# The down product of an MLP by seven products of quadrants: operands prepared in the stage before and kept in DRAM

## The chip, the cores and the metric

The kernel runs on one core of one Trainium2 chip. The core has five engines with queues of their own: TensorE (PE in the profile, PEld its weight loads), VectorE (DVE), ScalarE (ACT), GpSimd (POOL) and SyncE (SP). Transfers between DRAM and on-chip memory are issued from the queues of SP, ACT and POOL. The metric is the device time of one execution in microseconds.

## The reference

One decoder layer on 2048 tokens of width 1024. The part around the change is the gated MLP, with a depthwise convolution of width 3 over the tokens ahead of the activation (D_FF = 2816 = 22 x 128):

```python
h = h + jnp.concatenate([att, pool], axis=-1) @ w_out[i]
hn = _rmsnorm(h, ln_ffn[i])
up = _causal_dwconv(hn @ w_up[i], conv_w[i], conv_b[i])
gate, val = jnp.split(up, 2, axis=-1)
h = h + (jax.nn.silu(gate) * val) @ w_down[i]
g = jax.nn.sigmoid(_rmsnorm(h, ln_ple[i]) @ w_ple_gate[i])
h = h + g * (p[i] @ w_ple[i])
```

Ahead of it stand the input projection, a dilated sliding-window attention and a multi-scale pooling; behind it a last RMSNorm. All numbers are float32.

## The kernel before

Everything is kept transposed: features on the 128 partitions, tokens along the row. The 2048 tokens are four chunks of 512 (`CH`) or two halves of 1024.

**Split products.** TensorE multiplies in the type fp32r. `split` writes a number as a high part (ScalarE casts it, L84) and a low part (a subtraction on VectorE or GpSimd, L85), and `mm3` makes of one product three matmuls: high x high (L89), low x high (L90), high x low (L91). Each is 128x128 weights by 128x512 tokens.

**Up product** (930 to 1782 us of the profiled execution). For one half and one f (one of 22 blocks of 128 columns, for gate and value together) it multiplies two 2 x 2 block matrices by seven products in place of eight, in Winograd's form: the operands are quadrants a11, a12, a22 of the normed input, sums s1 to s4 of its quadrants, quadrants b11, b21, b22 of the weights and sums t1 to t4. Such a (half, f) is a *turn*: 7 x 4 x 3 = 84 matmuls (`product`, L1315). The split inputs of a half stay on chip in pools `opa` and `opb`. The sums t are made by GpSimd in the first half and kept in DRAM for the second. `prepare` norms the inputs of a half, makes s1 to s4 and stores them to DRAM (tiles `nt`); `Refill` fetches them again around the change of halves (the *half boundary*, turns `NF - 1`, `NF` and `NF + 1`), some fetches ahead, and splits them (`L1371`, `L1372`). A turn's products go into the banks ua, ub, uc; VectorE adds them up in `ug` and `uv` (`add`, L1338). One turn later the convolution (L1328 to L1335), ScalarE's silu and a product on VectorE (L1512) make `yg`, 128 x 1024, which is stored to `g.act`.

**Down product** (1782 to 2273 us). A loop over four chunks of tokens (c) and 22 blocks f; for each, 512 KB of weights and 256 KB of activations are loaded (`rd`, `ra`, SP's queue) and split, and `mm3` adds to eight output tiles of 128 x 512 (`dn`). The eighth output lags by `wait` = 5 blocks. A chunk closes with `closed(j)`: the old h, loaded from DRAM, plus the bank, stored to `h2`, and its square for the statistics of the next norm. The first three pairs of weights and activations are loaded and split by `first_units` inside the last turns of the up product.

**Gate phase** (2273 to 2519 us). The gate's and the embedding's products, the last norm and the output.

**What sets the order.** Within each engine's queue the instructions stand in the order written, with semaphores between engines; a buffer of a pool is taken again when its last reader is done. Inside the up product the place is given by slots: `after(slot)` is called seven times a turn, and `splits(slot)` puts the weights' splits behind certain products. In the down product `ahead(n + 3)` and `act_ahead(n + 3)` issue loads and splits three units ahead.

## Time and profile before

| | us |
|---|---|
| runs: lowest, median, highest of 3 | 2516.77, 2523.27, 2527.26 |
| profiled execution | 2522.12 |
| its span in the profile | 2519.8 |
| granted TensorE clock, mean | 0.98 |
| TensorE busy | 2407.5 (96% of the span) |
| VectorE, ScalarE, GpSimd busy | 1588.8, 1108.6, 515.7 |
| HBM read and written | 290.01 MB and 131.89 MB |

A row of a timeline has the start and the duration in us, the engine, line and operation, output<-inputs, shapes, and in brackets how long the engine was idle just before it and what it had waited for. A row of a group has the total of busy time, the mean of one instruction in ns, and the group's idle time by releaser. A row of windows has, for a stretch of time, the busy time and (x) instructions of each engine, the granted TensorE clock, the busy share of the DMA engines and what they moved. A row of DMA issues has the queue, the count, the size of one and the median time from issue to landing in us.

### The profile page before, as it was taken

To read this page: it belongs to the slowest core of one execution; us is meant where nothing else is said; L and a number is where in the kernel's file an instruction comes from. 1 tells how busy PE (TensorE), PEld (TensorE's weight loads), DVE (VectorE), ACT (ScalarE), POOL (GpSimd) and SP (SyncE) were. 2 spreads that over 40 slices of the span, in tenths; PEclk is the share of its full clock that TensorE was granted. 3 is DMA by queue.
4 is the path that set the end of the run, shared out by engine and by line. 5 is a ranking of instruction groups with operands and counts; after the bars stand their busy time and mean duration, and the time that the engine had idled before them with its cause. 6 is when DMAs were issued, how large, how long until landed. Compare 5 with 4: busy or idle time off the path is not lost.

```text
span 2519.8 us, 31897 instructions
## 1 busy us (share of the span) xinstructions
PE 2407.5 (96%) x11515; PEld 2022.4 (80%) x11515; DVE 1588.8 (63%) x2416; ACT 1108.6 (44%) x1923; POOL 515.7 (20%) x423
## 2 busy tenths in 40 slices
PE   8999998888779999999999999999999999999998
PEld 7888887777767877888887888888788888887888
DVE  6635427777774467888888666666535374435755
ACT  5423326887751135544446444444323242323322
POOL 3312221053430023333340000000122222221000
PEclk9999999999879999999999999999999999999999
DMA  7534358687646674555556334333546464635332
GB/s 240 174 120 180 142 178 248 166 193 180 164 164 221 223 252 167 167 177 181 175 194 211 122 117 138 121 114 117 191 134 222 149 219 150 208 122 173 124 105 88
DMA packets 209052, 424.08 MB, mean 168 GB/s; under 512 B 42464, under 2 KB 68896, under 8 KB 205824
## 3 DMA queue, kind: packets, MB, share of 16 engines
q1 hardware_dynamic: 170576, 368.41, 46.4%
q0 software_dynamic: 18672, 25.88, 3.1%
q10 hardware_dynamic: 19648, 27.77, 3.1%
q8 instruction: 90, 1.47, 0.2%
q14 instruction: 66, 0.54, 0.1%
HBM read 290.01 MB, written 131.89 MB: 167 GB/s over the span
## 4 chain that ended last, share of the span: by engine, by line
PE 79%; DMA 6%; DVE 6%; issue 3%; ACT 2%; POOL 0%; SPq 0%; ACTq 0%; POOLq 0%; DVEq 0%
PE ua L1315 18%; PE uc L1315 9%; PE dn L90 6%; PE dn L91 6%; PE dn L89 6%; PE ub L1315 4%; PE z L91 4%; PE z L89 4%; PE z L90 4%; PE o L89 2%; PE o L91 2%; PE o L90 2%; PE gp L89 2%; PE gp L91 2%; PE gp L90 2%
## 5 line engine op out<-in xcount | busy, mean ns | idle before, releaser
L89 PE MATMUL dn<-ah,hd 128*128 128x512 f32 x704 | 275.3, 391 | 2.8 <-ACT ah L84 2.8
L90 PE MATMUL dn<-al,hd 128*128 128x512 f32 x704 | 274.9, 391 | 1.7 <-DVE al L85 1.7
L91 PE MATMUL dn<-ah,ld 128*128 128x512 f32 x704 | 274.6, 390 | 0.0
L85 POOL TENSOR_TENSOR ld<-rd,hd 128x1024 fp32r<-128x1024 f32 x42 | 100.9, 2403 | 812.8 <-ACT hd L84 812.8
L84 ACT CAST hd<-rd 128x1024 fp32r<-128x1024 f32 x88 | 92.5, 1052 | 266.3 <-PE dn L90 230.9
L85 DVE TENSOR_TENSOR al<-ra,ah 128x512 fp32r<-128x512 f32 x88 | 116.8, 1330 | 136.0 <-ACT ah L84 136.0
L89 PE MATMUL z<-hnh,wh 128*128 128x512 f32 (+1 forms) x480 | 170.3, 355 | 9.9 <-ACT hnh L252 5.8
L90 PE MATMUL z<-hnl,wh 128*128 128x512 f32 (+1 forms) x480 | 170.0, 354 | 2.7 <-DVE hnl L253 2.6
L91 PE MATMUL z<-hnh,wl 128*128 128x512 f32 (+1 forms) x480 | 169.9, 354 | 2.3 <-POOL wl L85 1.7
L89 PEld LDWEIGHTS dn<-ah,hd 128*128 128x128 f32 x704 | 132.7, 188 | 31.0 <-ACT ah L84 3.2
L90 PEld LDWEIGHTS dn<-al,hd 128*128 128x128 f32 x704 | 132.7, 188 | 29.8 <-DVE al L85 2.2
L91 PEld LDWEIGHTS dn<-ah,ld 128*128 128x128 f32 x704 | 132.7, 189 | 27.4
L85 DVE TENSOR_TENSOR wu<-ru,wu 128x1024 fp32r<-128x1024 f32 x88 | 127.4, 1448 | 0.0
L155 DVE TENSOR_TENSOR acc<-acc,sq 128x512 f32<-128x512 f32 (+1 forms) x125 | 90.2, 722 | 47.6 <-ACT sq L154 34.6
L1315 PE MATMUL uc<-a22h,wu 128*128 128x512 f32 x352 | 115.7, 389 | 1.8 <-DVE uv L1338 1.8
L1315 PE MATMUL ua<-s2h,wu 128*128 128x512 f32 x352 | 115.8, 390 | 1.1 <-ACT ug L1452 1.1
L1315 PE MATMUL uc<-s3h,wu 128*128 128x512 f32 x352 | 116.2, 390 | 0.3 <-ACT s3h L1371 0.3
L1315 PE MATMUL ub<-a12h,wu 128*128 128x512 f32 x352 | 115.9, 390 | 0.3 <-ACT a12h L1371 0.3
L1315 PE MATMUL ua<-s4h,wu 128*128 128x512 f32 x352 | 115.5, 389 | 0.0
L1315 PE MATMUL ua<-s1h,wu 128*128 128x512 f32 x352 | 115.5, 389 | 0.0
L1315 PE MATMUL ua<-a11h,wu 128*128 128x512 f32 x352 | 115.5, 389 | 0.0
L85 DVE TENSOR_TENSOR ld<-rd,hd 128x1024 fp32r<-128x1024 f32 x46 | 56.2, 1223 | 89.1 <-ACT hd L84 89.1
(317 smaller groups left out, 6474.4 us busy)
## 6 DMA issues: line engine op xcount, KB each, us to landing
rd<-in_w_down_dram SPq DMA_DIRECT2D x88, 512.0 KB, 3.6
ru<-in_w_up_dram SPq DMA_DIRECT2D x66, 512.0 KB, 4.1
ra<-act SPq DMA_DIRECT2D x88, 256.0 KB, 3.8
act<-yg SPq DMA_DIRECT2D x43, 512.0 KB, 3.1
wr<-in_w_in_dram SPq DMA_DIRECT2D x64, 256.0 KB, 4.0
nt<-h SPq DMA_DIRECT2D x56, 256.0 KB, 3.9
h<-h SPq DMA_DIRECT2D x56, 256.0 KB, 5.6
td<-t SPq DMA_DIRECT2D x22, 512.0 KB, 2.6
```

What stands on the lines that cost most here:

```text
L84: nc.scalar.copy(hi, src)
L85: (low or nc.gpsimd).tensor_tensor(lo, src, fp(hi), op=ALU.subtract)
L89: nc.tensor.matmul(ps, wh, ah, start=first, stop=False)
L90: nc.tensor.matmul(ps, wh, al, start=False, stop=False)
L91: nc.tensor.matmul(ps, wl, ah, start=False, stop=last)
L155: nc.vector.tensor_tensor(acc[:, :n], acc[:, :n], sq[:, :n], op=ALU.add)
L1315: nc.tensor.matmul(pst, x[:, ksl], y, start=first and k == 0 and n == 0, stop=k == HK - 1 and n == 2, skip_group_check=True)
```

## The change

The down product becomes, for each half of 1024 tokens, seven products of quadrants like the up product's. Its rows are two chunks of tokens, its columns two halves of the 1024 outputs, and the sum over f is cut into the pairs (q, q + 11), q = 0 to 10. A *unit* is now one pair in one product: 12 matmuls on 256 KB of weights and 256 KB of activations. The seven products follow one another in `SEQ`, each over all 11 pairs, in two sets of four banks, A and B; some products go on adding to a bank that an earlier one has begun, and after each product its four banks are added to h as they stand.

The activations' quadrants and sums are made in the up product: the turns go in pairs (q, q + 11), and after the second one of a pair `results` stores a11, a12 and a22 and puts four subtractions or additions on VectorE for s1 to s4, stored to `g.oq`. The sums of the down weights are made by GpSimd in 11 turns of the second half (`down_sums`), with loads and stores on its own queue, and kept in `g.dd`. The normed inputs of `prepare` and `Refill` have four buffers where they had six, the fetches ahead are four and six instead of six and ten, and `prepare` for the second half begins in turn 3. The stores of the last pair, a11's apart, go to GpSimd's queue.

```diff
-        turns = [(half, f) for half in range(2) for f in range(NF)]
+        turns = [(half, f) for half in range(2) for q in range(NP) for f in (q, q + NP)]
...
-                        t[q] = pool.tile([P, CH], F32, tag="nt", bufs=6, name="nt")
+                        t[q] = pool.tile([P, CH], F32, tag="nt", bufs=nnt, name="nt")
...
-        FETCH = (("nt", 6), ("inv", 2), ("dg", 2))
+        FETCH = (("nt", 4), ("inv", 2))
...
-            nc.sync.dma_start(raw, rows(w_down, n))
+            nc.sync.dma_start(raw, w_down[n * P : (n + 1) * P, :CH])
...
+        def keep(half, p, q, t):
+            (nc.gpsimd if half and q == NP - 1 and p != "a11" else nc.sync).dma_start(g.oq[half][p][q], t)
+
+        def results(pr):
+            if pr.f < NP:
+                keep(pr.half, "a11", pr.f, pr.yg[:, lo_])
+                first_f[0] = pr.yg
+                return
+            q, half, one, two = pr.f - NP, pr.half, first_f[0], pr.yg
+            keep(half, "a12", q, two[:, lo_])
+            keep(half, "a22", q, two[:, hi_])
+            x = fp(fb.tile([P, CH], F32R, tag="dg", bufs=2, name="x"))
+
+            def sums_13():
+                nc.vector.tensor_tensor(x, one[:, hi_], two[:, hi_], op=ALU.add)
+                keep(half, "s1", q, x)
+                nc.vector.tensor_tensor(one[:, hi_], one[:, lo_], one[:, hi_], op=ALU.subtract)
+                keep(half, "s3", q, one[:, hi_])
+
+            def sum_2():
+                nc.vector.tensor_tensor(x, x, one[:, lo_], op=ALU.subtract)
+                keep(half, "s2", q, x)
+
+            def sum_4():
+                nc.vector.tensor_tensor(two[:, lo_], two[:, lo_], x, op=ALU.subtract)
+                keep(half, "s4", q, two[:, lo_])
+
+            sums.extend([[0, sums_13], [2, sum_2], [4, sum_4]])
...
+        def down_sums(q):
+            b = []
+            for r in (w_down[q * P : (q + 1) * P, :], w_down[(q + NP) * P : (q + NP + 1) * P, :]):
+                for x in range(2):
+                    t = fb.tile([P, CH], F32, tag="nt", bufs=4, name="nt")
+                    nc.gpsimd.dma_start(t, r[:, x * CH : (x + 1) * CH])
+                    b.append(t)
+
+            def rest():
+                b11, b12, b21, b22 = b
+                for n, (o, x, y) in enumerate(((b11, b12, b11), (b12, b22, b12), (b22, b22, b11), (b21, b21, b22))):
+                    nc.gpsimd.tensor_tensor(o, x, y, op=ALU.subtract)
+                    nc.gpsimd.dma_start(g.dd[q][("t1", "t3", "t2", "t4")[n]], o)
...
-            refill = Refill(0, ("a12", "s3", "a22"), 6)
+            refill = Refill(0, ("a12", "s3", "a22"), 4)
...
-                    (nc.gpsimd if over else nc.sync).dma_start(g.act[prev.f][:, prev.half * 1024 : prev.half * 1024 + 1024], prev.yg)
+                    results(prev)
...
+                if over:
+                    unit[4]()
+                    while sums:
+                        due_sums()
...
+        SEQ = (
+            ("a11", "b11", True, True, (0, 0)),
+            ("a12", "b21", False, True, (0, 0)),
+            ("s2", "t2", True, False, (1, 0)),
+            ("s3", "t3", False, True, (1, 1)),
+            ("s1", "t1", True, False, (1, 1)),
+            ("a22", "t4", False, False, (1, 0)),
+            ("s4", "b22", True, False, (0, 1)),
+        )
+        order = [(half, n, q) for half in range(2) for n in range(len(SEQ)) for q in range(NP)]
...
+                rw = fd.tile([P, CH], F32, tag="rw", bufs=4, name="rw")
+                nc.sync.dma_start(rw, weights(SEQ[x][1], q))
+                ra = fd.tile([P, CH], F32, tag="ra", bufs=4, name="ra")
+                nc.sync.dma_start(ra, g.oq[half][SEQ[x][0]][q])
+                w = wtile()
+                split(nc, w[:, :CH], w[:, CH:], rw, nc.vector)
...
+                split(nc, ah, al, ra, nc.vector)
...
+        for n, (half, x, q) in enumerate(order):
+            pa, wb, chain, starts, (row, col) = SEQ[x]
+            mine = "AB"[(half + (not chain)) % 2]
...
+            ahead(n + 4)
+            if n >= len(order) - 8 and n % 2 == len(order) % 2 and len(gates) < NW:
+                gates.append(load_w(rows(w_gate, len(gates)), f"g{len(gates)}", nc.vector))
+            if x in (0, 2, 3, 6) and q in (2, 4, 6, 8):
+                j = (q - 2) // 2
+                ht = fd.tile([P, CH], F32, tag="h", bufs=18, name="h")
+                c = 2 * half + row
+                nc.sync.dma_start(ht, g.h1[4 * col + j][:, c * CH : (c + 1) * CH])
...
+            for j in range(4):
+                js = slice(j * P, (j + 1) * P)
+                mm3(nc, banks[mine][j], wh[:, js], wl[:, js], ah, al, starts and q == 0, q == NP - 1, not starts)
+                if q == NP - 1:
+                    ht = htiles[half, row, col, j]
+                    nc.vector.tensor_tensor(ht, ht, banks[mine][j], op=ALU.add)
+                    if x in (1, 4, 5, 6):
+                        c = 2 * half + row
+                        nc.scalar.dma_start(g.h2[4 * col + j][:, c * CH : (c + 1) * CH], ht)
```

The rows below are instructions in the order of an engine's queue: line, operation, output<-inputs, shape. From L1342 of the kernel before on, the lines of the changed one are 4 and more higher; where before has `add` at L1338, the changed one has it at L1342, and its L1338 is a row of the convolution.

VectorE at the half boundary, the kernel before: the low parts of the refilled inputs (`s4l`, `a22l`) stand between the turn's own work.

```order
L1372 TENSOR_TENSOR s4l_12502<-nt,s4h_12501 128x512
L1338 TENSOR_TENSOR uv<-uv,uc 128x512
L1512 TENSOR_TENSOR yg<-yg,yv 128x1024
L85 TENSOR_TENSOR wu<-ru_12135,wu 128x1024
L85 TENSOR_TENSOR wu<-t_12323,wu 128x512
L1372 TENSOR_TENSOR a22l_12533<-nt,a22h_12532 128x512
L1372 TENSOR_TENSOR a22l_12537<-nt,a22h_12536 128x512
L1372 TENSOR_TENSOR a22l_12562<-ninv,a22h_12561 128x512
L1372 TENSOR_TENSOR a22l_12566<-ninv,a22h_12565 128x512
L1328 SCALAR_TENSOR_TENSOR yv<-uv,vec,yv 128x1023
```

The same place with the change; `x` is the tile of s1 and s2, `yg` the results of the pair.

```order
L1376 TENSOR_TENSOR s4l_12774<-ninv,s4h_12773 128x512
L1342 TENSOR_TENSOR uv<-uv,uc 128x512
L1581 TENSOR_TENSOR yg<-yg,yv 128x1024
L85 TENSOR_TENSOR wu<-ru_12395,wu 128x1024
L85 TENSOR_TENSOR wu<-t_12587,wu 128x512
L1376 TENSOR_TENSOR a22l_12807<-nt,a22h_12806 128x512
L1376 TENSOR_TENSOR a22l_12811<-nt,a22h_12810 128x512
L1418 TENSOR_TENSOR x<-yg 128x512
L1420 TENSOR_TENSOR yg<-yg 128x512
L1376 TENSOR_TENSOR a22l_12840<-nt,a22h_12839 128x512
L1376 TENSOR_TENSOR a22l_12844<-nt,a22h_12843 128x512
L1332 SCALAR_TENSOR_TENSOR yv<-uv,vec,yv 128x1023
```

Two of the pair's sums stand between the second and the third `a22l`.

VectorE where the up product ends, the kernel before: the convolution and the product of the last turn, and the splits of the down product's units three and four (`ld`, `al`).

```order
L1328 SCALAR_TENSOR_TENSOR yg<-ug,vec,yg 128x1023
L85 TENSOR_TENSOR ld_3_15458<-rd_3_15455,hd_3_15457 128x1024
L1329 SCALAR_TENSOR_TENSOR yg<-ug,vec,yg 128x1022
L1334 SCALAR_TENSOR_TENSOR yg<-halo,vec,yg 128x1
L1335 SCALAR_TENSOR_TENSOR yg<-halo,vec,yg 128x2
L1512 TENSOR_TENSOR yg<-yg,yv 128x1024
L85 TENSOR_TENSOR ld_5_15526<-rd,hd_5_15525 128x1024
```

With the change, from the same product on:

```order
L1581 TENSOR_TENSOR yg<-yg,yv 128x1024
L1418 TENSOR_TENSOR x<-yg 128x512
L1420 TENSOR_TENSOR yg<-yg 128x512
L85 TENSOR_TENSOR wu<-rd,wu 128x512
L85 TENSOR_TENSOR al<-ra,ah 128x512
L1424 TENSOR_TENSOR x<-x,yg 128x512
L1428 TENSOR_TENSOR yg<-yg,x 128x512
L85 TENSOR_TENSOR wu<-rw,wu 128x512
L85 TENSOR_TENSOR al<-ra,ah 128x512
```

The fifth unit's two splits stand between the pair's first two sums and its last two, and the sixth unit's (`rw`) behind all four.

SP's queue at the same place, with the semaphores that each transfer waits for (DMASW: transfers issued by GpSimd, DMAHW: by SP or ACT). Before:

```order
L1544 DMA rd<-in_w_down_dram 128x1024 [waits DMAHW6_49,DMAHW3_49,DVE_49]
L1544 DMA rd<-in_w_down_dram 128x1024 [waits DMAHW7_49,DMAHW5_49,Pool_49]
L1559 DMA ra<-act_208 128x512 [waits DMAHW0_49,DVE_49]
L1559 DMA ra<-act_209 128x512 [waits DMAHW1_49]
L1614 DMA h<-h_227 128x512 [waits DVE_49]
L1559 DMA ra<-act_210 128x512
```

With the change; `rg` are the gate's weights, `rd` the fifth unit's weights:

```order
L1386 DMA rd<-in_w_down_dram 128x512 [waits DMAHW2_49,DMAHW0_49,DVE_49]
L954 DMA rg_19694<-in_w_gate_dram 128x1024 [waits DMAHW6_49,DMAHW1_49,DVE_49]
L954 DMA rg_19748<-in_w_gate_dram 128x1024 [waits DMAHW0_49,DVE_49]
L1630 DMA rw<-in_w_down_dram 128x512 [waits DMAHW3_49]
L1632 DMA ra<-oq0a_210 128x512 [waits DMASW2_49,DMASW1_49,DMAHW4_49,DMASW0_49,Pool_49]
L1676 DMA h<-h_403 128x512 [waits DMAHW5_49,DMASW7_49,DVE_49]
L1630 DMA rw<-in_w_down_dram 128x512 [waits DMASW2_49]
L1632 DMA ra<-oq0a_211 128x512 [waits DMAHW7_49]
```

Two loads of the gate's weights now stand ahead of the sixth unit's, and the first load of h, which waits for a store of GpSimd's queue and for VectorE, ahead of the seventh's.

More of the change, by code (lines that the diff above doesn't have):

```diff
@@ L1520, in phase_rest @@
         pctx.close()
-        wait = 5
-        NX = 3
         dctx = ExitStack()
@@ L1635, in phase_rest @@
         aux[0] = db
-        ahead(len(order))
-        wg = [units.pop(("g", 0, k)) for k in range(NW)]
+        wg = gates
         wg += [load_w2(db, rows(w_gate, k), f"wg{k}", nc.vector) for k in range(NW, KD)]
@@ L1799, in tile_layer @@
     g.td = per(NF, [P, S], F32, "td")
-    g.act = per(NF, [P, S], F32, "act")
+    g.oq = [{p: per(NF // 2, [P, CH], F32, f"oq{h}{p}") for p in ("a11", "a12", "a22", "s1", "s2", "s3", "s4")} for h in range(2)]
+    g.dd = [{p: dr.tile([P, CH], F32, tag=f"dd{q}{p}", name=f"dd{q}{p}") for p in ("t1", "t2", "t3", "t4")} for q in range(NF // 2)]
     g.h1 = per(KD, [P, S], F32, "h1")
```

198 lines of the change are left out of this document (98 added, 100 removed).

## The prediction

> **What bounds the kernel now.** I read the page's busy line and its chain first, then the stages one by one, then the groups of the down product and the DMA issues.
>
> ```profile
> PE 2407.5 (96%) x11515; PEld 2022.4 (80%) x11515; DVE 1588.8 (63%) x2416; ACT 1108.6 (44%) x1923; POOL 515.7 (20%) x423
> ...
> PE 79%; DMA 6%; DVE 6%; issue 3%; ACT 2%; POOL 0%; SPq 0%; ACTq 0%; POOLq 0%; DVEq 0%
> ```
>
> TensorE is busy for 96% of the span and carries 79% of the chain. So fewer matmuls shorten the time, wherever nothing else becomes late. The stages, in order the first and second half of the up product, the down product, the gate phase, and then a stretch with the heaviest traffic of the down product:
>
> ```profile
> core 0: us, PE busy (x) PEld busy (x) DVE busy (x) ACT busy (x) POOL busy (x), PEclk, DMA share, GB/s
> 925.00:1358.00 433.00, 427.06 (x1872) 349.86 (x1871) 360.35 (x366) 215.34 (x270) 149.80 (x84) 1.00 0.53 179
> 1358.00:1784.00 426.00, 424.20 (x1870) 350.60 (x1869) 299.02 (x375) 213.06 (x264) 0.00 (x0) 1.00 0.39 129
> 1784.00:2273.00 489.00, 483.74 (x2134) 399.66 (x2133) 227.05 (x216) 161.50 (x215) 109.01 (x47) 0.99 0.55 179
> 2273.00:2519.00 246.00, 233.07 (x1261) 201.25 (x1259) 143.88 (x244) 77.81 (x139) 22.60 (x18) 0.98 0.36 119
> 2030.00:2060.00 30.00, 29.22 (x133) 24.06 (x132) 23.15 (x25) 15.90 (x24) 8.78 (x4) 1.00 0.88 290
> ```
>
> All four stages are TensorE's, at a granted clock of 0.98 to 1.00. The down product takes 489 us with some 5 us of idle TensorE, so only the number of its matmuls is to be had there.
>
> ```profile
> L89 PE MATMUL dn<-ah,hd 128*128 128x512 f32 x704 | 275.3, 391 | 2.8 <-ACT ah L84 2.8
> ...
> L84 ACT CAST ah<-ra 128x512 fp32r<-128x512 f32 x88 | 53.7, 615 | 13.5 <-DMA ra<-act 13.5
> ...
> L85 DVE TENSOR_TENSOR al<-ra,ah 128x512 fp32r<-128x512 f32 x88 | 116.8, 1330 | 136.0 <-ACT ah L84 136.0
> ```
>
> The row shows 704 matmuls, a third of the three forms, 2112 in all. Its 391 ns is not the price of one: 2112 x 0.391 = 826 us would not fit into 489 us, since matmuls overlap. The price is the step from one to the next. A turn of the up product has 7 x 4 x 3 = 84 matmuls of the same shape, and VectorE's same add comes back one turn later:
>
> ```profile
> 1160.12 0.69 DVE L1338 TENSOR_TENSOR ug<-ug,ub 128x512 f32<-128x512 f32 x1 [1.94 <-PE ub L1315]
> ...
> 1179.16 0.69 DVE L1338 TENSOR_TENSOR ug<-ug,ub 128x512 f32<-128x512 f32 x1 [1.41 <-PE ub L1315]
> ```
>
> (1179.16 - 1160.12) / 84 = 0.2267 us. By it the down product is 2112 x 0.2267 = 478.8 us; the rest of the 489 us is the stall at its start and its statistics.
>
> **Removed matmuls.** Seven products of 11 pairs, 4 outputs and 3 split terms are 924 matmuls in a half, 1848 in both: 264 fewer, as the order of TensorE's rows also has it. 264 x 0.2267 = 59.9 us, **-59.9**. A unit (one pair in one product) is 12 matmuls, 2.72 us.
>
> **Can the loads and splits keep up with 2.72 us?** Before, 24 matmuls (5.44 us) needed 768 KB; now 12 need 256 KB of weights and 256 KB of activations, 524,288 / 2.72 = 193 GB/s. Weights and activations were 88 x 0.786 = 69 MB of the stage's 179 x 489 = 87.5 MB; with 154 x 0.524 = 81 MB instead it is 99 MB in some 430 us, 231 GB/s, and by the stage's own share 0.55 x 231/179 = 0.71. The stretch at 2030 carried 290 GB/s at a share of 0.88 with TensorE busy for 29.2 of 30 us.
>
> ```profile
> rd<-in_w_down_dram SPq DMA_DIRECT2D x88, 512.0 KB, 3.6
> ...
> ra<-act SPq DMA_DIRECT2D x88, 256.0 KB, 3.8
> ...
> h<-h SPq DMA_DIRECT2D x56, 256.0 KB, 5.6
> ...
> mh<-mh POOLq DMA_DIRECT2D x12, 256.0 KB, 2.7
> ...
> qll<-ql SPq DMA_DIRECT2D x16, 512.0 KB, 14.3
> ```
>
> A buffer is taken from the issue to the landing (3.8, at worst h's 5.6) and 0.62 + 0.69, with the hop between them 1.4 us, for cast and subtraction, 5.2 to 7.0 us; four buffers allow 10.9. The splits, without GpSimd now, are 2 x 0.615 on ScalarE and 2 x 0.69 on VectorE in 2.72 us. That VectorE's `al` shows 1330 ns is GpSimd's doing, which leaves (0.69 in a row at 1802.68 below, without it). The closing adds rise from 32 to 56, 24 x 0.69 = 17 us of VectorE, beside TensorE, and each has a whole product (30 us) before its bank is used again. I take **0**; the ends are 0 and the second rival's price.
>
> The Trainium skill speaks against such loads: "DMA: Bandwidth & Descriptors", section "Rules for kernel authors", wants 128 partitions and at least 1 MiB per DMA for full bandwidth. Its section "Anatomy of one DMA — SWDGE (gpsimd) path" gives 2.0 us + bytes/436e3 on GpSimd's queue, by which I estimate 2.6 us for 256 KB and, one after another, 308 x 2.6 = 801 us. This trace agrees that half the size does not halve the landing (3.6 and 3.8 us), and not that they go one after another: 7.4 us of landings fitted into each 5.44 us. By the page the stage would be 801 us; by the rows the term is 0, and the page's case goes with rival 2.
>
> **The start of the down product.** Now its first matmul is at 1782.48 and it stalls 2.81 + 1.67 = 4.5 us for the fourth unit:
>
> ```profile
> 1782.48 0.39 PE L89 MATMUL dn<-ah,hd 128*128 128x512 f32 x1
> ...
> 1799.74 0.79 PE L89 MATMUL dn<-ah,hd 128*128 128x512 f32 x1 [2.81 <-ACT ah L84]
> 1802.20 0.80 PE L90 MATMUL dn<-al,hd 128*128 128x512 f32 x1 [1.67 <-DVE al L85]
> ```
>
> VectorE at that place:
>
> ```profile
> 1786.19 1.22 DVE L85 TENSOR_TENSOR ld<-rd,hd 128x1024 fp32r<-128x1024 f32 x1
> ...
> 1793.10 2.52 DVE L1512 TENSOR_TENSOR yg<-yg,yv 128x1024 f32<-128x1024 f32 x1 [1.19 <-ACT yg L1502]
> ...
> 1802.68 0.69 DVE L85 TENSOR_TENSOR al<-ra,ah 128x512 fp32r<-128x512 f32 x1 [0.54 <-ACT ah L84]
> ```
>
> With the change four units are ready, so the fifth is needed at 1782.5 + 4 x 2.72 = 1793.4. On VectorE the last product `yg<-yg,yv` comes 1.75 us earlier (ahead of it stand two splits of 0.69 instead of two of 1.22 and one of 0.69), so at 1791.35, and ends at 1792.6 without GpSimd beside it, then x and s3 to 1794.0, then the fifth unit's splits to 1795.3: a stall of 1.8. The sixth unit's load stands on SP's queue behind two loads of gate weights, which wait for the split buffers of units four and five; it is issued at about 1795.7 and ready at 1795.7 + 3.8 + 1.4 = 1800.9, needed at 1797.9: 3.0. The seventh's stands behind the first load of h, which waits for the last s2's store on GpSimd's queue (s1's store at 1794.3, landing 2.7 by `mh`, sum, store, landing 2.7: about 1801); 1801 + 3.8 + 1.4 = 1806.2 to 1806.8 against 1803.6: 3.2. Together 8.0 for 4.5: **+3.5**. Ends: 0 with landings of 2.6, +11 if all of them take h's 5.6.
>
> **The half boundary.** VectorE has no gap there, and two of its splits already end late or nearly so:
>
> ```profile
> 1376.87 0.50 PE L1315 MATMUL ua<-s4l,wu 128*128 128x512 f32 x1 [1.68 <-DVE s4l L1372]
> ...
> 1383.21 1.29 DVE L1372 TENSOR_TENSOR a22l<-ninv,a22h 128x512 fp32r<-128x512 f32 x2
> ```
>
> The fourth sum of the pair before lengthens the 1.68 by 0.7; the sums x and s3 of the last pair (1.2) and it put the last two `a22l` 1.8 us later, ready at 1385.6, needed at 1384.0 after a11's product: 1.6. **+2.3**, between 0.7 and 4. A matmul that waits on TensorE is not made up for later.
>
> **The first refill** (six fetches ahead become four). ScalarE waits there already, and TensorE with it:
>
> ```profile
> 947.35 0.62 ACT L1371 CAST s3h<-nt 128x512 fp32r<-128x512 f32 x1 [5.25 <-DMA nt<-op0s]
> ```
>
> Two fetches less ahead means an issue up to one slot (2.7 us) later behind the same 5.25: **+1**, from -1 to +3.
>
> **The sums in the up product.** In each second turn of a pair VectorE gets four more 128x512, 4 x 0.69 = 2.8 us. By the stage rows its idle time in the first half is (433 - 360) / 22 = 3.3 us a turn; the two adds above alone waited 1.94 and 1.41 us for TensorE. The light turn after it has the same again, and adds are late by at most a product (2.7 us) before a bank is missed. In the second half it idles (426 - 299) / 22 = 5.8 us a turn, but GpSimd's 44 subtractions are new there. In the first, 149.8 us of GpSimd went with 360 us of VectorE against 299 without; 44 of 149.8 / 84 = 1.8 us are 78, so 61 x 78/149.8 = 32 us more, 2.9 in each of 11 turns, and 2.9 + 2.8 stand against 5.8. **0**; up to 16 (1.5 us in each of 11 turns). The stores (1.75 MB for a pair, 1 MB before) run in 38 us at shares of 0.39 to 0.53: 0. Six of the last pair's seven stores move from SP's queue to GpSimd's: none but the h load above waits for them.
>
> **The gate phase.** Its weights come up inside the last eight units and its last closing has four adds instead of a train of eight: **0**, -3 to +3.
>
> **Sum.** -59.9 + 3.5 + 2.3 + 1 = -53.1. The profiled execution took 2522.1, so 2469.0; the median of the runs is 1.2 us above it: **2470**.
>
> **Rivals.** (1) VectorE falls behind in the second turns of the first half, because GpSimd slows its sums as it slows the splits there: 1 to 2 us in each of 11 turns, 2481 to 2491. For it: 2.8 us against 3.3, which contention (the 1330 ns of `al` against 690) would turn; against it: the light turn after. (2) The other side: the down product waits for its loads. The point is a cycle of 12.2 us per buffer (4 x (2.72 + 52/154)); above it the matmuls saved are spent. With `qll`'s 14.3 us (14.3 + 1.3)/4 = 3.9 us a unit, 154 x 3.9 = 601, and 2522 - 491 + 601 = 2632. For it: four pairs of 256 KB in flight, more requests; against it: 3.8 us at share 0.55, and the stretch at 290 GB/s. In part it gives 2491 to 2510. (3) The start is covered, and its 4.5 us go too: 2452 to 2460. That the matmuls do not fall is excluded by the order.
>
> **Chances.** The forecast 0.72 (its own range 2460 to 2482), rival 1 0.10, rival 3 0.05, loads late in part 0.03, about as before 0.05, slower 0.05. Less than 0.5% (2511 to 2536) can't be told from no change here. Faster 0.90, same 0.05, slower 0.05. The range takes the forecast, rival 1 and half of rival 3: 2455 to 2491.
>
> **What would show it.** Down product near 1848 x 0.2267 + 8 = 427 us plus statistics, with no wait for `rw` or `ra` after its first 25 us; the landing of `rw` and `ra` under 6 us; three stalls of 1.8, 3.0 and 3.2 us at its start; `s4l` at 2.4 and `a22l` at 1.6 us at the boundary; up turns still at 19.04 us. Wrong it would be by landings above 9 us in the down product, or by turns of 20 us where the sums are.

## The result, and the profile after

The changed kernel takes 2463.97 us (median of 4 runs, 2457.80 to 2468.53) against 2522.39 (4 runs, 2516.77 to 2527.26): the ratio is 0.9774, with a 95% interval from 0.9755 to 0.9793. It was forecast at 2470, from 2455 to 2491. The profiled execution took 2463.29 us, span 2461.2. Its busy line, a form of the down product's matmuls, and the loads:

```profile
PE 2345.0 (95%) x11251; PEld 1969.5 (80%) x11251; DVE 1723.8 (70%) x2705; ACT 1147.7 (47%) x2055; POOL 528.9 (21%) x515
...
L89 PE MATMUL dn<-ah,wu 128*128 128x512 f32 x616 | 240.8, 391 | 5.3 <-ACT ah L84 5.3
...
rw<-in_w_down_dram SPq DMA_DIRECT2D x61, 256.0 KB, 4.0
...
h<-h SPq DMA_DIRECT2D x56, 256.0 KB, 5.2
```

264 matmuls fewer (11515 to 11251), each group of the down product 616 where it had 704, and more work on VectorE and ScalarE. The stages by windows:

```profile
core 0: us, PE busy (x) PEld busy (x) DVE busy (x) ACT busy (x) POOL busy (x), PEclk, DMA share, GB/s
925.00:1358.00 433.00, 428.12 (x1876) 351.29 (x1876) 394.68 (x408) 217.40 (x271) 155.10 (x84) 1.00 0.59 195
1358.00:1784.00 426.00, 419.32 (x1839) 344.18 (x1838) 360.05 (x416) 207.95 (x259) 114.76 (x132) 1.00 0.61 203
1784.00:2214.00 430.00, 422.57 (x1864) 348.56 (x1863) 267.79 (x420) 204.16 (x350) 6.10 (x9) 1.00 0.72 235
```

The down product moves 235 GB/s at a share of 0.72 (231 and 0.71 were forecast). The second half of the up product has lost some 5 us of TensorE (424.2 to 419.3).

Windows cut at fixed times mix stages a little, so the balance below goes by starts of matmuls: the first of the up product, the first and the last of the down product, the last of all.

```profile
1788.33 0.39 PE L89 MATMUL dn<-ah,wu 128*128 128x512 f32 x1
...
2220.69 0.39 PE L91 MATMUL dn<-ah,wu 128*128 128x512 f32 x1
```

The table does this for each run, from its profiled execution. "Over" is what the turns take beyond 19.04 us each: the 22 turns of the first half, the two at the half boundary, and the others of the second half.

| kernel | up product | first half over | boundary over | second half over | down product | gate phase |
|---|---|---|---|---|---|---|
| before | 851.8 | 8.9 | 2.4 | 0.0 | 490.2 | 239.7 |
| changed | 858.1 | 8.1 | 4.8 | 4.7 | 432.4 | 233.3 |
| e1 eighth product | 861.3 | 7.9 | 6.0 | 7.0 | 492.7 | 233.2 |
| e2 two buffers | 859.2 | 9.7 | 4.9 | 4.0 | 439.9 | 233.9 |
| e3 half more loads | 862.7 | 9.5 | 6.2 | 6.5 | 433.8 | 233.2 |
| e4 start unit | 861.1 | 10.7 | 5.4 | 4.6 | 433.8 | 233.2 |
| e5 start memory | 858.2 | 8.1 | 5.7 | 3.9 | 427.1 | 233.3 |
| e6 light turns | 861.8 | 8.0 | 5.6 | 7.7 | 426.3 | 233.3 |
| e7 no subtractions | 854.3 | 8.2 | 5.6 | 0.0 | 432.9 | 233.2 |
| e8 no sums | 856.5 | 10.7 | 5.4 | 0.0 | 430.7 | 233.5 |
| e9 even turns | 865.0 | 11.6 | 5.7 | 7.2 | 427.2 | 233.2 |
| e10 gates late | 862.4 | 9.5 | 4.8 | 7.5 | 432.8 | 233.2 |
| e11 no sums, deep | 851.7 | 8.8 | 2.4 | 0.0 | 430.8 | 234.1 |
| e12 other tile | 856.2 | 7.8 | 5.2 | 2.8 | 426.9 | 233.2 |

From before to changed: up product +6.3, down product -57.9, gate phase -6.4, the rest (0.4 ahead of the first matmul, 0.1 behind the last) -0.5, together -58.6, which is the difference of the spans. Each row is one execution. The rows that have the same code in a stage, or nearly so, show how far one execution differs from the next there. For changed, e1 to e6, e9 and e10 it is 7.9 to 11.6 us over in the first half (5.8 to 9.6 of it in the first turn), 4.8 to 6.2 at the boundary and 3.9 to 7.7 in the second half, and the changed kernel's own execution stands near the low end of each. In the gate phase it is less than 1 us.

At the start of the down product TensorE's waits in the changed kernel are three, on units five, six and seven, as forecast:

```profile
1801.35 0.50 PE L90 MATMUL dn<-al,wu 128*128 128x512 f32 x1 [1.75 <-DVE al L85]
...
1808.27 0.62 PE L89 MATMUL dn<-ah,wu 128*128 128x512 f32 x1 [4.13 <-ACT ah L84]
1814.34 0.49 PE L89 MATMUL dn<-ah,wu 128*128 128x512 f32 x1 [1.22 <-ACT ah L84]
```

SP's queue beside them: the two loads of the gate's weights take from 1792.75 to 1801.05, and the sixth unit's `rw` comes behind them; the load of h goes out at 1808.35, and the seventh's `rw` behind it.

```profile
1792.75 8.30 SPq L954 DMA_DIRECT2D rg<-in_w_gate_dram  x2
1801.10 0.60 SPq L1630 DMA_DIRECT2D rw<-in_w_down_dram  x1
...
1808.35 0.33 SPq L1676 DMA_DIRECT2D h<-h  x1
1808.72 0.42 SPq L1630 DMA_DIRECT2D rw<-in_w_down_dram  x1
```

In the up product, behind its first turn, five of TensorE's waits of over 0.5 us are new, and a sixth, on `s4l`, stood at the boundary before too (1.68 us). Three are at the boundary, three in the second half:

```profile
1363.73 0.50 PE L1319 MATMUL ua<-s2h,wu 128*128 128x512 f32 x1 [0.92 <-ACT ug L1520]
1376.82 0.50 PE L1319 MATMUL ua<-s4l,wu 128*128 128x512 f32 x1 [1.65 <-DVE s4l L1376]
1385.24 0.50 PE L1319 MATMUL uc<-a22l,wu 128*128 128x512 f32 x1 [0.87 <-DVE a22l L1376]
...
1479.69 0.50 PE L1319 MATMUL uc<-a22h,wu 128*128 128x512 f32 x1 [0.53 <-DVE uv L1342]
1551.68 0.50 PE L1319 MATMUL ua<-s4h,wu 128*128 128x512 f32 x1 [0.56 <-ACT uv L1567]
1559.32 0.50 PE L1319 MATMUL uc<-a22h,wu 128*128 128x512 f32 x1 [1.90 <-DVE uv L1342]
```

The forecast had the one on `s4l` at 2.4 and the one on `a22l` at 1.6; the first, behind a copy of ScalarE, and the last three, in which VectorE is late, it had at nothing. The last three stand in the stretch in which GpSimd subtracts:

```profile
1385.00:1562.00 177.00, 173.69 (x761) 142.46 (x761) 166.43 (x164) 80.15 (x98) 113.60 (x130) 1.00 0.79 269
1562.00:1784.00 222.00, 221.95 (x979) 183.48 (x978) 167.21 (x217) 107.37 (x132) 0.00 (x0) 1.00 0.43 142
```

The program writes the 44 subtractions into 11 turns, up to turn 34 of turns 0 to 43. GpSimd runs ahead of that: the first starts at 1389.5, the last at 1554.7, in turn 31, and behind them it has nothing to do up to the down product. VectorE is busy for 166 of 177 us in that stretch, and for 167 of 222 us behind it, where no turn is late.

### The profile page after: what moved, and what is told of

Same layout as the page of the kernel before. It is cut to its first block, busy times and chain, and to the rows that moved or that the text cites. A ratio compares the mean times of both kernels' runs of the same rounds, so it can differ in the third digit from the quotient of the medians.

```text
span 2461.2 us, 32489 instructions
## 1 busy us (share of the span) xinstructions
PE 2345.0 (95%) x11251; PEld 1969.5 (80%) x11251; DVE 1723.8 (70%) x2705; ACT 1147.7 (47%) x2055; POOL 528.9 (21%) x515
## 4 chain that ended last, share of the span: by engine, by line
PE 73%; DVE 10%; DMA 8%; issue 3%; ACT 2%; POOL 0%; SPq 0%; DVEq 0%; POOLq 0%; ACTq 0%
PE ua L1319 15%; PE uc L1319 7%; PE dn L90 5%; PE dn L89 5%; PE dn L91 5%; PE ub L1319 4%; PE z L91 4%; PE z L89 4%; PE z L90 4%; PE o L91 2%; PE o L89 2%; PE o L90 2%; PE gp L89 2%; PE gp L90 2%; PE gp L91 2%
## 5 line engine op out<-in xcount | busy, mean ns | idle before, releaser
L89 PE MATMUL dn<-ah,wu 128*128 128x512 f32 x616 | 240.8, 391 | 5.3 <-ACT ah L84 5.3
L90 PE MATMUL dn<-al,wu 128*128 128x512 f32 x616 | 240.6, 391 | 2.1 <-DVE al L85 2.0
L91 PE MATMUL dn<-ah,wu 128*128 128x512 f32 x616 | 240.2, 390 | 0.0
L85 DVE TENSOR_TENSOR al<-ra,ah 128x512 fp32r<-128x512 f32 x154 | 105.9, 690 | 109.0 <-ACT ah L84 108.8
L84 ACT CAST ah<-ra 128x512 fp32r<-128x512 f32 x154 | 95.2, 621 | 143.1 <-PE dn L91 133.9
L110 POOL TENSOR_TENSOR pw<-ms,mhalf 128x4 f32<-128x4 f32 (+1 forms) x18 | 17.9, 995 | 636.3 <-ACT ms L108 636.3
L89 PEld LDWEIGHTS dn<-ah,wu 128*128 128x128 f32 x616 | 115.9, 188 | 30.3 <-ACT ah L84 6.2
L90 PEld LDWEIGHTS dn<-al,wu 128*128 128x128 f32 x616 | 116.0, 188 | 27.1 <-DVE al L85 3.2
L91 PEld LDWEIGHTS dn<-ah,wu 128*128 128x128 f32 x616 | 116.0, 188 | 24.2
L85 DVE TENSOR_TENSOR wu<-ru,wu 128x1024 fp32r<-128x1024 f32 x88 | 133.4, 1516 | 1.8 <-ACT wu L84 1.8
L85 DVE TENSOR_TENSOR wu<-rw,wu 128x512 fp32r<-128x512 f32 x149 | 101.1, 688 | 23.5 <-ACT wu L84 23.4
L89 PEld LDWEIGHTS z<-hnh,wh 128*128 128x128 f32 x480 | 94.0, 196 | 21.3 <-ACT hnh L252 5.8
```

What stands on the lines that cost most here:

```text
L84: nc.scalar.copy(hi, src)
L85: (low or nc.gpsimd).tensor_tensor(lo, src, fp(hi), op=ALU.subtract)
L89: nc.tensor.matmul(ps, wh, ah, start=first, stop=False, skip_group_check=again)
L90: nc.tensor.matmul(ps, wh, al, start=False, stop=False, skip_group_check=again)
L91: nc.tensor.matmul(ps, wl, ah, start=False, stop=last, skip_group_check=again)
L110: nc.gpsimd.tensor_tensor(pw[:, :nj], ms[:, :nj], g.mhalf[:, :nj], op=ALU.pow)
```

## The experiments

Kernels e1 to e4 shared one chip and its runs of the kernel before, e5 to e8 another set, e9 to e11 another; e12 ran by itself. A ratio is always to the kernel before, and e7, e8 and e11 ran once.

**e1: an eighth product.** It closes nothing, and its result is not used.

```diff
             ("s4", "b22", True, False, (0, 1)),
+            ("a11", "b11", False, True, (0, 1)),
         )
...
-                if q == NP - 1:
+                if q == NP - 1 and x < 7:
```

> The changed kernel with an eighth product of 11 units in each half (a11 times b11 once more, into the free set of banks, added to nothing): 264 matmuls more, the number of the kernel before, in the new staging; 22 more units of loads and splits come with them. Theory (the matmuls are the gain, 0.2267 us each, and everything that the new staging adds is hidden but for some 2 us): 2464 + 60 = 2524 us, 2519 to 2529, level with the kernel before. Rival (a part of the 58 us came from elsewhere, such as GpSimd's splits that are gone): the extra product then costs less than 50 us, under 2514. Rival (loads near their limit): over 2535, with waits for rw or ra.

2527.1 us, ratio 1.0020 (1.0006 to 1.0033). The down product takes 492.7 us, 60.3 more than the changed kernel's: 60.3 / 264 = 0.228 us a matmul, against the 0.2267 of the prediction. With 2112 matmuls each, the new staging's down product is 2.5 us longer than the old one's 490.2. So the matmuls are the gain, and the first theory stands; its rivals fall.

**e2: two buffers for rw and ra.**

```diff
-                rw = fd.tile([P, CH], F32, tag="rw", bufs=4, name="rw")
+                rw = fd.tile([P, CH], F32, tag="rw", bufs=2, name="rw")
```

(and the same for `ra`)

> The changed kernel with two buffers each for rw and ra in place of four. Theory (a buffer is taken for one issue, landing, cast and subtraction, about 0.4 + 4.0 + 0.62 + 0.69 + hops = 6.0 to 6.4 us, so two give a unit each 3.0 to 3.2 us against TensorE's 2.72): 154 x 0.3 to 0.5 = 45 to 75 us more, 2509 to 2539. Rival (the loads are far from any limit, landing shorter when fewer are in flight, 3.0 us or less): within 10 us of 2464.

2475.3 us, ratio 0.9816 (0.9793 to 0.9839); the down product is 7.6 us longer in its profile, which is of the fastest of its four runs (2469.3). Neither number held: the theory asked for 45 us and more. With fewer transfers in flight they land sooner, 3.4 us where it was 4.0,

```profile
rw<-in_w_down_dram SPq DMA_DIRECT2D x61, 256.0 KB, 3.4
```

so a buffer is taken for some 3.4 + 0.62 + 0.69 = 4.7 us and two of them allow 5.44. What it costs is, for the most part, one stretch, at 1870 to 1885, where the loads of h stand in the same queue (SP is 4.32 us busy with three of them) and TensorE waits 4.31 us. Four buffers cover such stretches.

**e3: a third load in each unit.** Nobody reads it.

```diff
                 nc.sync.dma_start(ra, g.oq[half][SEQ[x][0]][q])
+                more = fd.tile([P, CH], F32, tag="more", bufs=2, name="more")
+                nc.sync.dma_start(more, weights(SEQ[x][1], q))
```

> The changed kernel with a third load of 256 KB in each unit, which nobody reads: 40 MB more in the down product, 768 KB in 2.72 us, 235 x (101 + 40) / 101 = 328 GB/s where 290 at a share of 0.88 was seen. Theory (four buffers allow 10.9 us from issue to free): landings of 5 to 8 us, the stage up by 0 to 15 us, 2464 to 2479. Rival (the down product stands at the edge of what its loads can do, so that rival 2 of the prediction was close): 40 MB at 290 GB/s to the full, some 100 us or more in proportion to the bytes, over 2500.

2465.8 us, ratio 0.9770 (0.9748 to 0.9792), no more than the changed kernel. In the middle of its down product:

```profile
core 0: us, PE busy (x) PEld busy (x) DVE busy (x) ACT busy (x) POOL busy (x), PEclk, DMA share, GB/s
1850.00:2200.00 350.00, 348.60 (x1545) 288.19 (x1544) 217.96 (x342) 171.66 (x292) 2.78 (x2) 1.00 0.96 332
```

332 GB/s at a share of 0.96, landings of 4.4 to 5.2 us, and TensorE busy for 348.6 of 350 us. Rival 2 of the prediction was far off: the changed kernel's 239 GB/s in this window leaves room for 40% more.

**e4 and e5: the start of the down product.** e4:

```diff
+        def load_w(src, name, low=None, q=nc.sync):
...
-                gates.append(load_w(rows(w_gate, len(gates)), f"g{len(gates)}", nc.vector))
+                gates.append(load_w(rows(w_gate, len(gates)), f"g{len(gates)}", nc.vector, nc.gpsimd))
...
-                nc.sync.dma_start(ht, g.h1[4 * col + j][:, c * CH : (c + 1) * CH])
+                (nc.sync if n > NP else nc.gpsimd).dma_start(ht, g.h1[4 * col + j][:, c * CH : (c + 1) * CH])
...
                     unit[4]()
+                    first_units(5)()
```

> The changed kernel with three things moved at the start of the down product: the gate's weights and the first four loads of h on GpSimd's queue, and the sixth unit loaded and split like the first five, ahead of the last two sums. Theory (the stalls of 4.13 and 1.22 us there are the queue's and the sums', the 1.75 us of the fifth unit VectorE's own): the first two go, the third stays; 4 to 5.5 us less, 2458.5 to 2460, ratio to before 0.9752 to 0.9760. Rival (loads take that long to land there whatever stands ahead of them): 2464 with the same sum of stalls.

2468.8 us, ratio 0.9795 (0.9771 to 0.9819): not faster. The 4.13 and 1.22 us are gone, and one wait of 7.75 stands in their place, on the seventh unit. TensorE and SP in e4:

```profile
1818.37 0.80 PE L89 MATMUL dn<-ah,wu 128*128 128x512 f32 x1 [7.75 <-ACT ah L84]
```

```profile
1807.57 0.33 SPq L1631 DMA_DIRECT2D rw<-in_w_down_dram  x1
1813.92 0.33 SPq L1633 DMA_DIRECT2D ra<-oq0a  x1
```

No load stands ahead of them now, but they go out late. In the program these two wait for the store of s3, the instruction of s2, and the store of s2; the store of s3 lands at 1807.51, the store of s2 at 1813.87. With a sixth unit loaded in advance the loop asks for a tile of h before its first `rw` and `ra`; the pool lays tiles out in the order of the first request, so the 18 tiles of h took the memory that was long free, and `rw` and `ra` that of the last results. e5 puts the requests back in the order of the changed kernel:

```diff
-            ahead(n + 4)
+            ahead(max(n + 4, 7))
```

> The kernel of e4 with its first two units of the down product's loop asked for before the first h, so that the buffers of rw and ra lie in memory that is long free, and the 18 of h over the last results (in e4 it was the other way round). Theory (the 7.75 us stall of e4 was rw and ra waiting for the stores out of that memory): only the fifth unit's 1.75 us stays at the start; 5 us under the changed kernel, 2456 to 2461, ratio to before 0.974 to 0.976. Rival (the loads themselves are slow at that place): a stall of over 3 us stays for the seventh unit.

2459.9 us, ratio 0.9773 (0.9747 to 0.9799). The seventh unit's wait is gone; TensorE now waits for VectorE's splits alone,

```profile
1798.16 0.50 PE L90 MATMUL dn<-al,wu 128*128 128x512 f32 x1 [1.75 <-DVE al L85]
1805.79 0.50 PE L90 MATMUL dn<-al,wu 128*128 128x512 f32 x1 [1.90 <-DVE al L85]
1809.30 0.50 PE L90 MATMUL dn<-al,wu 128*128 128x512 f32 x1 [0.48 <-DVE al L85]
```

and the down product takes 427.1 us, 5.3 under the changed kernel. The memory was the cause in e4. The 5.3 us are shown by the stage; the ratio's interval is too wide to show them by itself, and the 1.90 and 0.48 us had not been expected.

**e7 and e8: which work makes the second half's turns longer.** e7 leaves out GpSimd's subtractions, e8 VectorE's sums:

```diff
-                    nc.gpsimd.tensor_tensor(o, x, y, op=ALU.subtract)
```

```diff
-                nc.vector.tensor_tensor(x, one[:, hi_], two[:, hi_], op=ALU.add)
-                keep(half, "s1", q, x)
...
+                keep(half, "s1", q, one[:, hi_])
```

(and so for s2 to s4)

> The changed kernel without GpSimd's 44 subtractions; what it loads it stores as it is, so loads and stores stay and the down weights' sums are wrong numbers. Theory (GpSimd beside VectorE is what makes VectorE late in the second half): VectorE's 360 us there fall to 330 or less and the three waits of 0.53, 0.56 and 1.90 us go; about 2461. Rival (VectorE's sums, or the transfers): VectorE stays over 350 us, the waits stay.

> The changed kernel without VectorE's sums s1 to s4 of the activations: the halves of the results are stored in their place, as many stores. Theory (the sums cost no more than the waits that the trace shows): the boundary's 0.92 and 0.87 us and the second half's 3.0 go, 4 to 5 us less, about 2459; the stall of 4.13 us at the start of the down product falls by the two sums and the store between them, 2 to 3 us. Rival (the sums cost more than the trace's waits show): under 2450.

e7 took 2455.2 us, e8 2461.6. In both the second half is 0.0 over, where nine executions with both had 3.9 to 7.7: each of the two alone is hidden, the two together are not. In e7 VectorE's busy time there falls from 360 to 322 us for as much work of its own:

```profile
1358.00:1784.00 426.00, 421.65 (x1856) 347.77 (x1856) 322.27 (x418) 209.35 (x260) 47.86 (x88) 1.00 0.60 201
```

The boundary stays at 5.4 to 5.6 us in both, so it does not need the sums, which the prediction had blamed, to be that late. Of e8's further expectations, the 4.13 us at the start did not fall: TensorE waits 5.75 there without the sums, though the fifth unit's wait falls to 0.62 and the seventh's goes, and all of them together fall from 7.33 to 6.37.

**e11: the boundary.** e8 with eight fetches ahead.

```diff
-        FETCH = (("nt", 4), ("inv", 2))
+        FETCH = (("nt", 4), ("inv", 2), ("dg", 2))
...
-                    refill = Refill(1, ("a11", "s2", "a12", "s1", "s3", "s4", "a22"), 6)
-                    for _ in range(6):
+                    refill = Refill(1, ("a11", "s2", "a12", "s1", "s3", "s4", "a22"), 8)
+                    for _ in range(8):
```

> The kernel of e8 (no sums of the activations) with eight fetches ahead at the half boundary in place of six. e8 has shown that without the sums the two boundary turns still take 5.4 us more than 2 x 19.04. Theory (there ScalarE waits for the refill's loads, since fewer are ahead): the two turns fall to 2.0 to 3.0 us over, as in the kernel before, and ScalarE's waits of 0.9 and 2.85 us for the loads go. Rival (something else in the boundary, such as GpSimd's queue or the order of turns): still over 4 us.

The boundary is back at 2.4 us, as in the kernel before (2460.9 us, one run). ScalarE's waits for the loads in e8,

```profile
1365.47 0.62 ACT L1375 CAST s1h<-nt 128x512 fp32r<-128x512 f32 x1 [0.90 <-DMA nt<-op1s]
1371.42 1.31 ACT L1375 CAST s3h<-ninv 128x512 fp32r<-128x512 f32 x2 [2.85 <-DMA ninv<-op1s]
```

are gone in e11. They are in the changed kernel too (1.43 and 1.43 us), and not in the kernel before. A late cast of the refill also makes the copies behind it on ScalarE late, which free TensorE's banks: that is the wait of 0.92 us at 1363.73 above. The changed kernel with its sums and eight fetches was not run.

**e6, e9 and e12: trying to move the two apart.** All three are built on e5.

```diff
# e6
-                    q = i - NF - 2
+                    q = (i - NF - 2 + 1) // 2 if i == NF + 2 or i % 2 and i > NF + 2 else -1
...
-            sums.extend([[0, sums_13], [2, sum_2], [4, sum_4]])
+            d = 2 if half == 0 and q == NP - 1 else 0
+            sums.extend([[d, sums_13], [d + 2, sum_2], [d + 4, sum_4]])
# e9
-                    q = i - NF - 2
+                    q = {24: 0, 25: 1}.get(i, (i - NF) // 2 if i > 25 and i % 2 == 0 else -1)
# e12
-                nc.vector.tensor_tensor(x, x, one[:, lo_], op=ALU.subtract)
-                keep(half, "s2", q, x)
+                nc.vector.tensor_tensor(one[:, lo_], x, one[:, lo_], op=ALU.subtract)
+                keep(half, "s2", q, one[:, lo_])
...
-            sums.extend([[0, sums_13], [2, sum_2], [4, sum_4]])
+            sums.extend([[0, sums_13], [0, sum_2], [2, sum_4]])
```

> The kernel of e5, with GpSimd's subtractions of the down weights in the turns where VectorE makes no sums (all but the first of 11), and the last pair's sums of the first half two slots later, behind the last a22l. Theory: the second half's waits of TensorE for VectorE (0.53 + 0.56 + 1.90 us in the changed kernel) go, and the a22l stall of 0.87 too; 3 to 4 us less than e5, 2452 to 2458. Rival (the waits come from VectorE's own sums): the three waits stay.

> The kernel of e5, with GpSimd's subtractions in the even turns only (and in one odd one): there VectorE has only the first two sums, at the turn's end, while the sums of s2 and s4 stand in slots 1 and 3 of the odd turns, in which e6 had put the subtractions by mistake. Theory (sums and subtractions at one time make VectorE late, neither alone): the second half's turns are all 19.04 us, 3 to 4 us less than e5 in its up product; 2453 to 2458. Rival (every turn with GpSimd beside VectorE is late, or the transfers are): turns over 19.04 us stay in the second half.

e6 took 2461.0 us (ratio 0.9764, 0.9736 to 0.9791), e9 2460.1 (0.9758, 0.9741 to 0.9775). Both theories missed: the second half is 7.7 and 7.2 us over, no better than where the subtractions stood. But neither edit moved the two apart. e6 puts the subtractions by mistake into the turns of s2 and s4, as e9's expectation says, and both edits change only the place in the program. Behind the boundary nothing ties GpSimd's queue to a turn: in the changed kernel it idles between its subtractions almost only for its own loads (the first row), and in e9, which places the last ones in turn 42, it is done in turn 31 all the same (the second and third):

```profile
L1454 POOL TENSOR_TENSOR nt<-nt 128x512 f32<-128x512 f32 x44 | 66.1, 1502 | 35.4 <-DMA nt<-in_w_down_dram 34.7
1385.00:1562.00 177.00, 172.05 (x751) 141.35 (x750) 162.49 (x162) 80.38 (x98) 110.24 (x132) 0.99 0.79 269
1562.00:1784.00 222.00, 222.00 (x980) 183.74 (x979) 167.91 (x216) 108.93 (x133) 0.00 (x0) 1.00 0.43 143
```

So the two runs say nothing about subtractions that are apart from the sums, and that stays untested. In e6 the a22l wait of the boundary did go, with the sums behind it, but the boundary as a whole stayed at 5.6. VectorE in e9, at the turn that lost 6 us:

```profile
1554.29 1.71 DVE L1424 TENSOR_TENSOR x<-x,yg 128x512 f32<-128x512 f32 x1 [6.33 <-DMA oq1s<-x]
1555.92 0.67 DVE L1342 TENSOR_TENSOR ug<-ug,uc 128x512 f32<-128x512 f32 x1
1556.52 2.18 DVE L85 TENSOR_TENSOR wu<-ru,wu 128x1024 fp32r<-128x1024 f32 x1
```

It stands for 6.33 us in the instruction of s2, which overwrites s1 and so waits for s1's store to land; GpSimd's loads go at the same time. Then it goes on beside GpSimd, 2.18 us for a split that takes 1.22 alone. The changed kernel's waits have a row for the same (us in total, times, the longest):

```profile
DVE x L1424 <- DMA oq1s<-x: 12.9, 10, 3.2
...
1547.57 0.69 DVE L1424 TENSOR_TENSOR x<-x,yg 128x512 f32<-128x512 f32 x1 [3.22 <-DMA oq1s<-x]
```

The longest of them, the second row, stands right ahead of TensorE's waits of 0.56 and 1.90 us.

e12 takes the wait away.

> The kernel of e5, with s2 written over a11 (whose store was issued a turn before) instead of over s1, and so made right behind s1 and s3; s4 two slots later. In the changed kernel, e5, e6 and e9 VectorE waits in the instruction of s2 up to 3.2 to 6.6 us for the store of s1 out of the same tile, and the late turns of the second half stand right behind these waits. Theory (that wait, with GpSimd beside VectorE afterwards, is what makes VectorE late): the second half's 21 turns add up to less than 1 us over 19.04 each (4.7 in the changed kernel, 3.9 in e5, 7.2 in e9); 3 to 4 us less than e5 in the same execution's up product, 2452 to 2458. Rival (GpSimd beside VectorE alone): 3 us or more over stay.

2455.4 us, ratio 0.9742 (0.9718 to 0.9766). One wait of a sum for a store is left in VectorE's rows (s4 for the store of a12, 1.0 us, at 1802 behind the last turn), and the second half is 2.8 us over: less than the 3.9 to 7.7 of the nine executions with sums over s1 beside the subtractions, more than the theory's 1, and hardly less than the rival's 3. So the store is likely a part, on one execution; e12 also makes s2 and s4 two slots earlier, and no run tells that from the store. The rest is one wait of 1.16 us and its after-effects, behind a stretch in which VectorE runs beside GpSimd:

```profile
1541.16 1.28 DVE L1332 SCALAR_TENSOR_TENSOR yv<-uv,vec,yv 128x1023 f32<-128x1023 f32 x1
...
1548.87 2.89 DVE L1332 SCALAR_TENSOR_TENSOR yg<-ug,vec,yg 128x1023 f32<-128x1023 f32 x1 [1.79 <-ACT yg L1328]
1551.79 2.19 DVE L1333 SCALAR_TENSOR_TENSOR yg<-ug,vec,yg 128x1022 f32<-128x1022 f32 x1
```

The last two take 1.28 us alone, as the first row shows. In e7 the waits for the store are as long (up to 6.34 us) and cost nothing. e12 has the lowest median of the kernels that leave nothing out; against the changed kernel the intervals of the two ratios overlap, so that it is faster is shown by the down product of its profile, 426.9 against 432.4, which it has from e5, and not by the ratios. Its up product, 856.2 against 858.1 to 865.0 in the nine, is the shortest of them by 1.9 us.

**e10: the gate's weights last.**

```diff
-            if n >= len(order) - 8 and n % 2 == len(order) % 2 and len(gates) < NW:
-                gates.append(load_w(rows(w_gate, len(gates)), f"g{len(gates)}", nc.vector))
```

> The changed kernel with the gate's weights split after the last unit of the down product, as the kernel before had it, in place of inside its last eight units. Theory (the gate phase is 6.4 us shorter in the changed kernel because these weights, and the loads queued behind them, come earlier): TensorE waits for wph or the gate's weights again and its clock dips after it, the gate phase back at 238 to 242 us; 2468 to 2474. Rival (the gate phase gained by something else, the last closings for one): it stays at 233 us, 2464.

2467.7 us, ratio 0.9792 (0.9776 to 0.9808); the gate phase stays at 233.2 us. Where the loop asks for these weights is not the reason. But the edit did not make the loads behind them late, so the theory's second half was not tested. The second set of the gate's weights goes out at 2222.60 in e10, 3.7 us ahead of the last matmul of the down product (2226.31), and so it does in the changed kernel (2216.99 against 2220.69). In the kernel before it goes out at 2279.12, 6.4 us behind that matmul (2272.72). The last load of the weights that `wph` is made of lands 20.4 and 20.5 us behind it in e10 and the changed kernel, 25.5 in the kernel before. That these loads come earlier fits the gain; why they do is a reading that was not tried: in the kernel before, the gate's weights share the two buffers `raw` with the down product's.

## Why the prediction was right

**The removed matmuls, -59.9.** Shown twice: the down product lost 57.9 us net, and e1's 264 matmuls cost 60.3. The step of 0.2267 us, from the up product's turns, was the right price.

**Loads and splits, 0.** Right: 0.72 of the DMA engines, a median landing of 3.7 us for `rw` and 3.3 for `ra` (the longest 6.6, just over the 6 that had been named), no wait after the first 27 us. e2 and e3 show the room: the buffer cycle in the prediction took landings as fixed, and they shorten when less is in flight. The rule on transfers of 1 MiB and more, in the Trainium skill's "DMA: Bandwidth & Descriptors", section "Rules for kernel authors", does not set the time here: in e3, transfers of 256 KB carried 332 GB/s. The 308 loads that were estimated at 801 us one after another fitted into 432 us.

**The start of the down product, +3.5.** Measured 1.75 + 4.13 + 1.22 + 0.23 = 7.33 us of waits against 4.48, +2.85. The fifth unit's 1.8 was met to 0.05 us; the sixth's was 4.13 where 3.0 stood (`rw` went out at 1801.10, 12.8 us after the first matmul, forecast 13.2, but landed in 5.8), and so the seventh's was shorter, 1.22 for 3.2.

**The half boundary, +2.3.** Measured +2.4, and the nearness is luck. The first of its two turns is 1.2 us longer, with the wait of 0.92 behind a copy of ScalarE, which the prediction did not have; `s4l`, forecast 0.7 later, waits 1.65 us for 1.68 before. The second is 1.2 us longer, with the 0.87 us on `a22l`, where the named step, the sums ahead of it, can have a part (in e6, with the sums behind it, that wait goes). But e8 keeps the boundary at 5.4 without any sum, and e11 returns it to 2.4 with two fetches more: the smaller depth alone is enough. The prediction had costed it at the first refill only. Other executions of this code had +2.4 to +3.8.

**The first refill, +1.** The first turn went from 4.7 to 6.0 us over, +1.3. In the eight other executions it was 5.8 to 9.6 over, so the size is not settled, and the upper end of +3 too low for some. But the first half as a whole is 0.9 us shorter in this execution: the prediction gave no price to `prepare` starting a turn later, and its turn, 22.8 us before, is now two of 19.57 and 20.02. These two are the same to 0.05 us in all runs and worth 2.3 us.

**The sums in the up product, 0.** Mis-sized: 4.7 us, all in the second half, where the working had found 5.8 us of idle time for 5.7 of work. It spread GpSimd's slowing over 11 pairs of turns and VectorE's idle time over 22 turns. In the trace all 44 subtractions run between 1389.5 and 1556, within nine turns, and VectorE has 10.6 of 177 us idle there and 55 of 222 behind. And it compared sums over a turn; what came late was one instruction that waits for a store (3.22 us at 1547.57), with GpSimd beside VectorE after it. Rival 1 had the first half as its place, and there was nothing.

**The gate phase, 0, -3 to +3.** Missed: -6.4. The wait on `wph` (2.76 us), which stood in the profile of before, and two smaller ones went, with the half clock behind them (below). The step that put this at nothing looked at the order of the instructions and not at when the loads behind the gate's weights land; that they land 5 us earlier is in the traces, why they do is open (e10).

Together the errors (-6.4 gate, -1.9 first half, -1.5 down product, +4.7 sums, -0.4 of small ones) are the 5.5 us between -53.1 and -58.6. Without the gate phase they cancel to 0.9 us, which is luck: the matmuls, the loads and the start were right by their mechanism, the boundary, the sums and the gate phase were not.

## What to carry to other kernels

Price a matmul by the step between matmuls in a full stretch, not by its mean duration, and a removed one is worth just that as long as its stage stays TensorE's. Work that is moved into the idle time of another stage has to fit instruction by instruction: a sum made in place waits for the store of what it overwrites, and everything behind it on its engine waits too. A place in the program is no place in time: look in the trace when an engine with little to wait for does its work, before moving that work by turns. When loads are moved or asked for earlier, look where their tiles lie: a new pool can put them over the last stage's results, and then they wait for stores that no line of the loop names.

## What the runs showed of the hardware

**A wait of TensorE costs more than the wait.** In the gate phase of the kernel before, TensorE is behind its wait for `wph` at 2299.29; from 2301.7 to 2305 its matmuls start every 0.42 to 0.43 us in place of 0.23:

```profile
2301.68 0.63 PE L89 MATMUL pl<-pph,wph 128*128 128x512 f32 x1
2302.11 0.63 PE L90 MATMUL pl<-ppl,wph 128*128 128x512 f32 x1
```

The windows over it (behind TensorE's busy time come the granted clock, the DMA share and GB/s):

```profile
2301.00:2303.00 2.00, 2.00 (x8) 0.61 1.04 396
2303.00:2305.00 2.00, 2.00 (x7) 0.54 0.70 267
2305.00:2307.00 2.00, 2.00 (x10) 1.00 0.02 5
```

The clock is 0.61 and 0.54, then 1.00. So the 3.6 us of waits there came with some 2.2 us of slow matmuls, and the stalls at the start of the down product with some 2.9 before and 3.0 after. The Trainium skill tells this in "TensorE: Matmul & The Clock Gate", "Part 1: The HAM clock gate": after an idle window of about 3.4 us the array runs at half its clock for such a window. The half agrees (0.42 against 0.23 us); here 2.8 us of waiting in a busier stretch were enough, and 2.33 us in e10 (at 1478.42; clock 0.50 from 1479.0 to 1482.4). Shorter ones do it in some executions and not in others: a wait of 1.91 us for `s4l` in e4 (at 1380.72) was followed by 3.4 us at 0.50, one of 1.90 us in e5 (at 1374.42) by a clock of 1.00. That is a part of what makes the boundary differ between executions.

**GpSimd slows only some of VectorE's work.** Beside it the convolution and splits take up to 2.2 to 2.9 us for 1.28 and 1.22, but the add from a bank does not change: in the changed kernel's up product all 132 take 0.67 to 0.69 us, and 12 of them lie wholly within one instruction of GpSimd. The Trainium skill's "GPSIMD Engine Reference", section "1. Specifications", names the shared interface to on-chip memory for instructions with two inputs there; the add reads one of its inputs from a bank, and the trace agrees.
